# Up projection in fp32r: the input's two parts as one 512-column moving operand, with an earlier start of the down projection's loads

## The chip, the cores and the metric

One NeuronCore of one Trainium2 chip runs the whole block in one launch. The metric is the device time of the program in microseconds (us), as the median of several runs.

## The reference, cut to what matters

```
h    = rms_norm(x, norm2) * (1 + sc2) + sh2          # 512 tokens, 2048 channels
gate, val = split(h @ w_up, 2)                       # 2048 -> 2 x 6144
gate = causal_dwconv(gate, ffn_conv_w, ffn_conv_b)   # 3 taps along the tokens
x    = x + g2 * ((gelu(gate) * val) @ w_down)        # 6144 -> 2048
return rms_norm(x, norm_final)
```

Ahead of it stands a mixer of about the same kind (an input projection of 4096 columns, a gated token mixer, a linear recurrence, an output projection). The six modulation vectors (sh1, sc1, g1, sh2, sc2, g2) are products of `silu(c)` with `w_ada`.

## The kernel before, in words

All products run on TensorE in float32r. Each float32 operand is cut in two parts, `hi` (the value rounded to float32r) and `lo` (what is left), and a product is the sum of three: hi weights by hi input, hi weights by lo input, lo weights by hi input. `round_up` (line 162, ScalarE) writes the hi part of 1024 weight columns into `wh`, `rest` (line 167, VectorE) the lo part into `wl`; each tag has three buffers.

The program is a list `steps`. A step takes one 512 KB block of weights. The loop at the end of the kernel works at step j: it issues the load for step j + 5, rounds the weights of step j + 2 on ScalarE, runs the small work that `put(j, fn, cost, half)` has hung on the step (half -1 first, 0 before VectorE's rest for step j + 2, 1 after it), and issues the step's matmuls. Every engine keeps this order, so an instruction that waits holds up all that stand behind it on its engine.

Steps up to 95 are the mixer. Steps 96 to 111 make the first four output columns of the up projection in the plain way (`mm_w`, lines 173 to 175). The other 44 columns f (128 gate and 128 value channels each) are made by a Strassen-like scheme: 2 x 2 blocks of the weights and of the input (low and high channels, first and second 256 tokens) give seven products P1 to P7 in place of eight. So there are 308 steps. In each, `go` runs over eight blocks of 128 input channels, and for each over the three part products (lines 875 to 877) of 256 columns, one token half. The moving operand `m` has hi and lo side by side: for P1, P2 and P4 a half of each of the two rows of an `h2` tile (tag `hp`), for P6, P5, P7 and P3 sums of the blocks that `combine` (lines 818 to 840) made in steps 104 to 111, in tiles `xs` and `sx`. The results go to banks x, z and y of PSUM, all of them to the first half of the bank.

In `column(f)`, t1 to t4 (VectorE, lines 910 to 922) form sums of weight blocks, and `after_p1` to `after_p3` take the products out of the banks, 256 columns at a time: ScalarE copies c1, u2, u3 and half of the gate, VectorE adds z + c1 (938), y + u3 (948), y + u2 (956). Then come the taps (806), gelu (969), the product with the value (959), and the store of the 256 KB result to `kept`.

The down projection follows from step J1, in two halves of four groups of twelve steps; a step is 24 matmuls of 512 columns (5.44 us). Its input is read back: `act_load` (256 KB into `yl`, three buffers) and `act_split` (lines 1051 and 1052: hi on ScalarE, lo on VectorE) into 16 `hp` tiles and 11 `dp` tiles. `g2_load` fetches one 1 MB block of `w_ada` into the only `araw` buffer in every second step, and `ada` (line 209, VectorE) reduces it to one column of the gate g2. At a group's end `settle` (line 979, VectorE) adds the four finished banks, times g2, to x2. There are six banks for these sums, so the next group can start on two and needs settle for the rest. From step J1 + 4 the tiles `araw`, `yl` and `dp` stand in a pool `back`, in the order in which they are first asked for.

## Time and profile before

| what | value |
|---|---|
| median of 3 runs | 2150.6 us (2147.19 to 2150.71) |
| the profiled execution's own time | 2149.32 us |
| its span, first to last instruction | 2147.6 us |
| TensorE busy | 2094.9 us (98%) |
| weight loads busy | 1861.4 us (87%) |
| VectorE busy | 1508.0 us (70%) |
| ScalarE busy | 875.0 us (41%) |
| mean granted TensorE clock | 0.989 |

The profiled execution takes 1.7 us more than its span, and lies 1.3 us below the median. Matmuls overlap in the records (a row's length is longer than the distance to the next start), so TensorE's pace is read from the starts. The same holds in a small way for VectorE and ScalarE.

### The profile page before, as it was taken

The page shows a single profiled execution, that of the slowest core. Times are in us where ns is not written, and L with a number is a line of the kernel's source. Part 1 is how long each engine was busy: PE and PEld are TensorE (multiplying, and loading weights), DVE is VectorE, ACT ScalarE, POOL GpSimd, SP SyncE. Part 2 cuts the span into 40 slices and gives each one's busy share as a digit, 9 for nine tenths or more (in the row PEclk, how much of TensorE's full clock was granted, in tenths as well). Part 3 has the DMA queues.
Part 4 walks back from the last instruction along what each step waited for, and adds up shares of the span by engine and source line. Part 5 has one row for each costly group of instructions (what it writes and reads, how often), then busy time and mean ns, then how long its engine had stood idle before and what let it go on. Part 6 is the DMA issues. An engine that isn't in the chain of part 4 may idle for free. (4 is left out here: it accounts for less than half of the span.)

```text
span 2147.6 us, 30757 instructions
## 1 busy us (share of the span) xinstructions
PE 2094.9 (98%) x12620; PEld 1861.4 (87%) x12620; DVE 1508.0 (70%) x1851; ACT 875.0 (41%) x1148; POOL 4.7 (0%) x12
## 2 busy tenths in 40 slices
PE   7999999999989999999999999999998999999996
PEld 4887778888768999999999999999997888888885
DVE  8999889787768777877877877877865444432333
ACT  5323775332234544544544444444452112222222
POOL 0000000000000000000000000000000000000000
PEclk8999999999999999999999999999999999999998
DMA  9876443679822333233233233233256555422222
GB/s 369 331 286 222 147 157 129 225 285 336 301 96 99 126 131 131 93 132 128 94 133 127 95 133 127 95 133 127 96 182 258 217 210 182 160 91 98 89 98 79
DMA packets 97069, 351.43 MB, mean 164 GB/s; under 512 B 12704, under 2 KB 12832, under 8 KB 84640
## 3 DMA queue, kind: packets, MB, share of 16 engines
q1 hardware_dynamic: 81520, 293.36, 38.3%
q10 hardware_dynamic: 15408, 56.11, 7.2%
q8 instruction: 99, 1.62, 0.3%
q14 instruction: 42, 0.34, 0.0%
HBM read 328.45 MB, written 20.97 MB: 163 GB/s over the span
## 5 line engine op out<-in xcount | busy, mean ns | idle before, releaser
L162 ACT CAST wh<-raw 128x1024 fp32r<-128x1024 f32 x340 | 356.9, 1050 | 694.4 <-PE mm L174 483.8
L167 DVE TENSOR_TENSOR wl<-raw,wh 128x1024 fp32r<-128x1024 f32 x340 | 416.0, 1224 | 238.4 <-ACT wh L162 235.8
L173 PE MATMUL mm<-hp,wh 128*128 128x512 f32 x1280 | 508.7, 397 | 15.2 <-DVE xs L979 5.8
L175 PE MATMUL mm<-hp,wl 128*128 128x512 f32 x1280 | 502.2, 392 | 3.1 <-DVE wl L167 3.1
L174 PE MATMUL mm<-hp,wh 128*128 128x512 f32 x1280 | 502.5, 393 | 0.8 <-DVE hp L234 0.8
L173 PEld LDWEIGHTS mm<-hp,wh 128*128 128x128 f32 x1280 | 242.7, 190 | 72.4 <-ACT hp L226 9.1
L877 PE MATMUL mm<-xs,wl 128*128 128x256 f32 x1056 | 299.1, 283 | 0.6 <-DVE wl L167 0.5
L875 PE MATMUL mm<-xs,wh 128*128 128x256 f32 x1056 | 298.9, 283 | 0.0
L876 PE MATMUL mm<-hp,wh 128*128 128x256 f32 x1056 | 298.9, 283 | 0.0
L877 PE MATMUL mm<-hp,wl 128*128 128x256 f32 x1056 | 298.8, 283 | 0.0
L875 PE MATMUL mm<-hp,wh 128*128 128x256 f32 x1056 | 298.8, 283 | 0.0
L876 PE MATMUL mm<-xs,wh 128*128 128x256 f32 x1056 | 298.8, 283 | 0.0
L175 PEld LDWEIGHTS mm<-hp,wl 128*128 128x128 f32 x1280 | 242.5, 189 | 55.1 <-DVE wl L167 4.4
L174 PEld LDWEIGHTS mm<-hp,wh 128*128 128x128 f32 x1280 | 242.5, 189 | 54.3 <-issue 2.4
L209 DVE SCALAR_TENSOR_TENSOR araw<-araw,crow 128x2050 f32<-128x2050 f32 (+1 forms) x96 | 219.8, 2291 | 44.0 <-DMA araw<-w_ada 44.0
L167 DVE TENSOR_TENSOR wl<-rawb,wh 128x1024 fp32r<-128x1024 f32 x132 | 161.7, 1225 | 76.7 <-ACT wh L162 76.7
L877 PEld LDWEIGHTS mm<-xs,wl 128*128 128x128 f32 x1056 | 202.7, 192 | 1.0 <-DVE wl L167 1.0
L875 PEld LDWEIGHTS mm<-hp,wh 128*128 128x128 f32 x1056 | 202.7, 192 | 0.0
L875 PEld LDWEIGHTS mm<-xs,wh 128*128 128x128 f32 x1056 | 202.7, 192 | 0.0
L876 PEld LDWEIGHTS mm<-hp,wh 128*128 128x128 f32 x1056 | 202.7, 192 | 0.0
L877 PEld LDWEIGHTS mm<-hp,wl 128*128 128x128 f32 x1056 | 202.7, 192 | 0.0
L876 PEld LDWEIGHTS mm<-xs,wh 128*128 128x128 f32 x1056 | 202.7, 192 | 0.0
(214 smaller groups left out, 2615.5 us busy)
## 6 DMA issues: line engine op xcount, KB each, us to landing
araw<-w_ada SPq DMA_DIRECT2D x64, 1024.5 KB, 5.9
raw<-w_dn SPq DMA_DIRECT2D x96, 512.0 KB, 3.4
raw<-w_us SPq DMA_DIRECT2D x88, 512.0 KB, 4.5
rawb<-w_us SPq DMA_DIRECT2D x88, 512.0 KB, 4.9
araw<-w_ada SPq DMA_DIRECT2D x32, 1025.0 KB, 7.2
raw<-w_in ACTq DMA_DIRECT2D x59, 512.0 KB, 4.0
raw<-w_out ACTq DMA_DIRECT2D x32, 512.0 KB, 6.1
act_kept<-fy SPq DMA_DIRECT2D x48, 256.0 KB, 2.2
```

What stands on the lines that cost most here:

```text
L162: A.copy(hi, raw)
L167: V.tensor_tensor(out=lo, in0=raw, in1=hi, op=SUB)
L173: PE.matmul(ps, w[0][:, cs], h[0], start=first, stop=False)
L174: PE.matmul(ps, w[0][:, cs], h[1], start=False, stop=False)
L175: return PE.matmul(ps, w[1][:, cs], h[0], start=False, stop=last)
L209: V.scalar_tensor_tensor(out=raw, in0=raw, scalar=1.0, in1=crow[:, :w], op0=MUL, op1=MUL, accum_out=mods[:, n:n + 1])
L875: PE.matmul(ps, hi[:, cs], m[:, 0, :], start=first, stop=False, skip_group_check=True)
L876: PE.matmul(ps, hi[:, cs], m[:, 1, :], start=False, stop=False, skip_group_check=True)
L877: PE.matmul(ps, lo[:, cs], m[:, 0, :], start=False, stop=last, skip_group_check=True)
```

## The change

In a product, the hi weights now multiply both parts of the input in one matmul of 512 columns: hi input into the lower half of the bank, lo input into the upper half. The lo weights still multiply the hi input, 256 columns into the lower half. So 24 matmuls of 256 columns become 8 of 512 and 8 of 256. The two halves of a bank have to be added in the end; since the scheme is linear, that is done once per column and output: all copies and adds out of the banks are twice as wide (c1, u2, u3, `gw`, `vw`), `gate` adds the halves of the gate, `value` those of the value.

Of the four sums of `combine`, the fourth goes into the upper half of an `h2` tile, which is free once the plain steps have read it; the `sx` tiles go. For that reason the combines move one step later, and the last two share step 111.

In the down projection the first four loaded results are split into `xs` tiles, `yl` has four buffers, nearly every load is issued two steps ahead of its split where it was one, and the blocks of `w_ada` are loaded at steps J1 + 5, 7, 9, 11, 13, 16, 19 and so on in place of J1 + 4, 6, 8 and so on. The buffer `araw` grows by 128 bytes. The core of the diff (the renamed helpers of `column` that only got wider are left out):

```diff
-            raw = sb("araw", 2 if pl is mid else 1, (P, D + (2 if pl is mid else 32)), pl=pl)
+            raw = sb("araw", 2 if pl is mid else 1, (P, D + (2 if pl is mid else 64)), pl=pl)
...
-            two = sb("sx", 8, (P, 2, HS), F32R, ffn) if k in (2, 3) else sb("xs", NXS, (P, 2, HS), F32R)
+            two = sb("xs", NXS, (P, 2, HS), F32R) if i < 3 else h2[k][2][:, :, upper]
...
-            put(UP0 + 8 + k, lambda k=k, rests=rests: rests.append(combine(k)))
-            put(UP0 + 8 + k, lambda rests=rests: rests[0](), 0.0, 1)
+            j = UP0 + 9 + min(k, 6)
+            put(j, lambda k=k, rests=rests: rests.append(combine(k)))
+            put(j, lambda rests=rests: rests[0](), 0.0, 1)
...
-            ps = of[f][b][:, lower]
+            ps = of[f][b]
+            both = ps.rearrange("p (a b) -> p a b", a=2)
...
-                PE.matmul(ps, hi[:, cs], m[:, 0, :], start=first, stop=False, skip_group_check=True)
-                PE.matmul(ps, hi[:, cs], m[:, 1, :], start=False, stop=False, skip_group_check=True)
-                PE.matmul(ps, lo[:, cs], m[:, 0, :], start=False, stop=last, skip_group_check=True)
+                PE.matmul(both, hi[:, cs], m, start=first, stop=False, skip_group_check=True)
+                PE.matmul(ps[:, lower], lo[:, cs], m[:, 0, :], start=False, stop=last, skip_group_check=True)
...
-            V.tensor_tensor(out=o["g"][:, lower], in0=o["z"][:, lower], in1=o["c1"], op=ADD)
+            V.tensor_tensor(out=o["gw"][:, :, lower], in0=two(o["z"]), in1=two(o["c1"]), op=ADD)
...
-            V.tensor_tensor(out=o["v"][:, upper], in0=o["y"][:, lower], in1=u3, op=ADD)
+            V.tensor_tensor(out=o["vw"][:, :, upper], in0=two(o["y"]), in1=two(u3), op=ADD)
...
+        def gate():
+            o["g"] = sb("fg", 1, pl=ffn)
+            V.tensor_tensor(out=o["g"], in0=o["gw"][:, 0, :], in1=o["gw"][:, 1, :], op=ADD)
...
-            V.tensor_tensor(out=o["v"][:, lower], in0=o["y"][:, lower], in1=o["u2"], op=ADD)
+        def value():
+            V.tensor_tensor(out=o["vw"][:, 0, :], in0=o["vw"][:, 0, :], in1=o["vw"][:, 1, :], op=ADD)
...
+        put(at_["P4"] + 2, gate)
+        put(at_["P3"] + 3, value, 0.0, 1)
...
-        yls[f] = sb("yl", 3, pl=room2[0] or ffn)
+        yls[f] = sb("yl", 4, pl=room2[0] or ffn)
...
-        two = pair() if f < 16 or 27 <= f < 43 else sb("dp", 11, (P, 2, S), F32R, room2[0])
+        if f < EARLY:
+            hi, lo = (sb("xs", NXS, dt=F32R) for _ in range(2))
+        else:
+            two = pair() if f < EARLY + 16 or EARLY + 26 <= f < EARLY + 42 else sb("dp", 10, (P, 2, S), F32R, room2[0])
...
-        if f < 27:
+        if f < EARLY + 26:
             j = J1 + f // 2
-            first, then = (j - 3, j - 2) if f > 5 else (J1 + (-6, -6, -6, -3, -2, -1)[f], J1 + (-4, -3, -2, -1, 0, 0)[f])
+            first, then = (j - 4, j - 2) if f >= 8 else (J1 - 6, J1 - 2 + f // 2) if f < 4 else (J1 - 4 + f // 2, J1 - 2 + f // 2)
...
-        put(J1 + 4 + 2 * k, lambda k=k: g2_load(k))
-        put(J1 + 5 + 2 * k, lambda: ada(*g2_loaded.pop()))
+        j = J1 + (5 + 2 * k if k < 4 else 1 + 3 * k)
+        put(j, lambda k=k: g2_load(k))
+        put(j + (0 if k == 3 else 1), lambda: ada(*g2_loaded.pop()), 0.0, 1)
```

VectorE's order in one column of the up projection, from the add that follows P3 to the rest of the weights of the next column's P4 (`wl` and `wh` are parts of weights, `mm` banks, `vt` constants). Before:

```order
L956 TENSOR_TENSOR fv_5397<-mm_5342,u_902_5336 128x256
L167 TENSOR_TENSOR wl_5500<-raw_5206,wh_5498 128x1024
L922 TENSOR_TENSOR rawb_5322<-rawb_5322,t_916_5447 128x1024
L938 TENSOR_TENSOR fg_5530<-mm_5502,c_913_5429 128x256
L806 SCALAR_TENSOR_TENSOR fy_5464<-fg_5304,vt,fy_5464 128x511
L167 TENSOR_TENSOR wl_5535<-raw_5256,wh_5532 128x1024
L806 SCALAR_TENSOR_TENSOR fy_5464<-fg_5304,vt,fy_5464 128x510
L167 TENSOR_TENSOR wl_5568<-raw_5449,wh_5565 128x1024
L959 TENSOR_TENSOR fy_5464<-fy_5464,fv_5397 128x512
L167 TENSOR_TENSOR wl_5599<-rawb_5322,wh_5596 128x1024
```

Now:

```order
L960 TENSOR_TENSOR vw_5349<-mm_5310,u_894_5304 128x2x256
L964 TENSOR_TENSOR fg_5426<-gw_5280 128x512
L167 TENSOR_TENSOR wl_5430<-raw_5194,wh_5424 128x1024
L923 TENSOR_TENSOR rawb_5294<-rawb_5294,t_908_5387 128x1024
L946 TENSOR_TENSOR gw_5452<-mm_5432,c_905_5373 128x2x256
L167 TENSOR_TENSOR wl_5456<-raw_5244,wh_5454 128x1024
L806 SCALAR_TENSOR_TENSOR fy_5428<-fg_5426,vt,fy_5428 128x511
L806 SCALAR_TENSOR_TENSOR fy_5428<-fg_5426,vt,fy_5428 128x510
L167 TENSOR_TENSOR wl_5482<-raw_5389,wh_5479 128x1024
L969 TENSOR_TENSOR vw_5349<-vw_5349 128x512
L972 TENSOR_TENSOR fy_5428<-fy_5428,vw_5349 128x512
L167 TENSOR_TENSOR wl_5506<-rawb_5294,wh_5503 128x1024
```

The three bank adds are two times 256 wide where they were 256, and the adds of lines 964 and 969 are new, so the same stretch has twelve instructions in place of ten.

VectorE's order where the plain steps end and the columns begin, from the rest of P2's weights in step 111 (`rawb` holds sums, line 838 makes their lo parts, `t` is a sum of weight blocks, and line 806 is a tap of the last two plain columns). Before:

```order
L167 TENSOR_TENSOR wl_5190<-rawb_5111,wh_5175 128x1024
L915 TENSOR_TENSOR t_885_5204<-rawb_5064,raw_4970 128x1024
L838 TENSOR_TENSOR xs_5182<-rawb_5177,xs_5182 128x256
L838 TENSOR_TENSOR xs_5184<-rawb_5177,xs_5184 128x256
L838 TENSOR_TENSOR xs_5186<-rawb_5177,xs_5186 128x256
L838 TENSOR_TENSOR xs_5188<-rawb_5177,xs_5188 128x256
L806 SCALAR_TENSOR_TENSOR fy_5224<-mm_4860,vt,fy_5224 128x511
L806 SCALAR_TENSOR_TENSOR fy_5224<-mm_4860,vt,fy_5224 128x510
```

Now:

```order
L167 TENSOR_TENSOR wl_5178<-rawb_5089,wh_5152 128x1024
L916 TENSOR_TENSOR t_877_5192<-rawb_5043,raw_4951 128x1024
L838 TENSOR_TENSOR xs_5159<-rawb_5154,xs_5159 128x256
L838 TENSOR_TENSOR xs_5161<-rawb_5154,xs_5161 128x256
L838 TENSOR_TENSOR xs_5163<-rawb_5154,xs_5163 128x256
L838 TENSOR_TENSOR hp_4611<-rawb_5154,hp_4611 128x256
L838 TENSOR_TENSOR xs_5171<-rawb_5166,xs_5171 128x256
L838 TENSOR_TENSOR xs_5173<-rawb_5166,xs_5173 128x256
L838 TENSOR_TENSOR xs_5175<-rawb_5166,xs_5175 128x256
L838 TENSOR_TENSOR hp_4614<-rawb_5166,hp_4614 128x256
L806 SCALAR_TENSOR_TENSOR fy_5216<-mm_4847,vt,fy_5216 128x511
L806 SCALAR_TENSOR_TENSOR fy_5216<-mm_4847,vt,fy_5216 128x510
```

Eight lo parts stand ahead of the taps in place of four, and four more instructions of a combine stand ahead of the first row.

VectorE's order at the end of the first group of the down projection (`dp` are split results, `araw` a block of `w_ada`, and the `xs` rows are settle). Before:

```order
L1052 TENSOR_TENSOR dp_15852<-yl_15832,dp_15852 128x512
L1052 TENSOR_TENSOR dp_15855<-yl_15834,dp_15855 128x512
L167 TENSOR_TENSOR wl_15860<-raw_15722,wh_15848 128x1024
L1052 TENSOR_TENSOR dp_15892<-yl_15874,dp_15892 128x512
L209 SCALAR_TENSOR_TENSOR araw_15858,mods<-araw_15858,crow 128x2049
L167 TENSOR_TENSOR wl_15896<-raw_15765,wh_15888 128x1024
L979 SCALAR_TENSOR_TENSOR xs_15662<-mm_15430,mods,xs_15662 128x512
L979 SCALAR_TENSOR_TENSOR xs_15706<-mm_15431,mods,xs_15706 128x512
```

Now:

```order
L209 SCALAR_TENSOR_TENSOR araw_13483,mods<-araw_13483,crow 128x2049
L1072 TENSOR_TENSOR dp_13560<-yl_13499,dp_13560 128x512
L1072 TENSOR_TENSOR dp_13563<-yl_13501,dp_13563 128x512
L167 TENSOR_TENSOR wl_13568<-raw_13432,wh_13556 128x1024
L209 SCALAR_TENSOR_TENSOR araw_13566,mods<-araw_13566,crow 128x2049
L994 SCALAR_TENSOR_TENSOR xs_13329<-mm_13097,mods,xs_13329 128x512
L994 SCALAR_TENSOR_TENSOR xs_13372<-mm_13098,mods,xs_13372 128x512
L994 SCALAR_TENSOR_TENSOR xs_13416<-mm_13099,mods,xs_13416 128x512
L994 SCALAR_TENSOR_TENSOR xs_13459<-mm_13100,mods,xs_13459 128x512
L1072 TENSOR_TENSOR dp_13603<-yl_13539,dp_13603 128x512
L1072 TENSOR_TENSOR dp_13606<-yl_13541,dp_13606 128x512
```

The splits of the group's end now stand behind settle, and the fourth block of `w_ada` is reduced right ahead of it, in the step of its load.

## Rows read from the trace of the kernel before

**Rows 1.** The page: busy us, share of the span, instructions.

```profile
PE 2094.9 (98%) x12620; PEld 1861.4 (87%) x12620; DVE 1508.0 (70%) x1851; ACT 875.0 (41%) x1148; POOL 4.7 (0%) x12
```

**Rows 2.** Busy time by stretch, up projection: stretch, length, engines, granted clock, DMA.

```profile
900.00:1100.00 200.00, 200.00 (x1669) 200.00 (x1668) 157.93 (x169) 98.64 (x130) 0.00 (x0) 1.00 0.34 117
```

**Rows 3.** Order of time, TensorE, up projection (101 matmuls): start, length, line, tiles.

```profile
1000.06 0.28 PE L877 MATMUL mm<-hp,wl 128*128 128x256 f32 x1
...
1012.06 0.28 PE L875 MATMUL mm<-xs,wh 128*128 128x256 f32 x1
```

**Rows 4.** The same, down projection: 25 matmuls on dp, then 16 on hp.

```profile
1640.25 0.40 PE L173 MATMUL mm<-dp,wh 128*128 128x512 f32 x1
...
1645.85 0.40 PE L173 MATMUL mm<-dp,wh 128*128 128x512 f32 x1
...
1799.89 0.39 PE L175 MATMUL mm<-hp,wl 128*128 128x512 f32 x1
...
1803.29 0.39 PE L175 MATMUL mm<-hp,wl 128*128 128x512 f32 x1
```

**Rows 5.** Groups by line, 650:1650 (last: 40:560): count, busy us, mean ns, idle before.

```profile
L162 ACT CAST wh<-raw 128x1024 fp32r<-128x1024 f32 x152 | 159.6, 1050 | 130.0 <-PE mm L876 103.0 <-issue 13.1 <-PE mm L174 12.7
L167 DVE TENSOR_TENSOR wl<-raw,wh 128x1024 fp32r<-128x1024 f32 x151 | 184.2, 1221 | 5.4 <-ACT wh L162 3.2
L814 DVE TENSOR_TENSOR fy<-mm,fy 128x512 f32<-128x512 f32 x4 | 2.8, 692 | 4.3 <-ACT fy L813 4.3
L332 ACT COPY xs<-mm 128x512 f32<-128x512 f32 x16 | 8.9, 588 | 1.6 <-PE mm L182 0.5 <-PE mm L175 0.4
```

**Rows 6.** Order of time, VectorE, within one column.

```profile
1007.81 0.42 DVE L938 TENSOR_TENSOR fg<-mm,c 128x256 f32<-128x256 f32 x1
```

**Rows 7.** Order of time where the columns begin: VectorE, last row TensorE.

```profile
691.26 0.48 DVE L825 SCALAR_TENSOR_TENSOR rawb<-xs,shsum,xs 128x256 f32<-128x256 f32 x1
...
695.24 1.42 DVE L838 TENSOR_TENSOR xs<-rawb,xs 128x256 fp32r<-128x256 f32 x4
696.58 1.53 DVE L806 SCALAR_TENSOR_TENSOR fy<-mm,vt,fy 128x511 f32<-128x511 f32 x2
...
702.76 1.23 DVE L167 TENSOR_TENSOR wl<-t,wh 128x1024 fp32r<-128x1024 f32 x1 [0.25 <-ACT wh L162]
...
704.04 0.39 PE L877 MATMUL mm<-xs,wl 128*128 128x256 f32 x1 [0.49 <-DVE wl L167]
```

**Rows 8.** Order of time, TensorE after two earlier waits (rows 549.28 to 553.28: 12 matmuls).

```profile
549.28 0.50 PE L173 MATMUL mm<-hp,wh 128*128 128x512 f32 x1 [2.70 <-DVE xs L382]
...
553.28 0.62 PE L175 MATMUL mm<-hp,wl 128*128 128x512 f32 x1
...
587.15 0.50 PE L175 MATMUL mm<-hp,wl 128*128 128x512 f32 x1 [1.69 <-DVE wl L167]
```

**Rows 9.** Busy time by stretch, right after the second of these waits.

```profile
587.00:589.00 2.00, 1.85 (x8) 1.54 (x9) 1.84 (x3) 0.00 (x0) 0.00 (x0) 1.00 0.38 115
```

**Rows 10.** Order of time, first group of the down projection: TensorE, ScalarE, VectorE.

```profile
1647.23 0.50 PE L175 MATMUL mm<-dp,wl 128*128 128x512 f32 x1 [0.74 <-DVE wl L167]
...
1653.61 0.39 PE L175 MATMUL mm<-hp,wl 128*128 128x512 f32 x1
1659.84 0.79 PE L173 MATMUL mm<-hp,wh 128*128 128x512 f32 x1 [5.85 <-DVE xs L979]
...
1663.28 0.39 PE L175 MATMUL mm<-hp,wl 128*128 128x512 f32 x1
...
1654.43 0.62 ACT L1051 CAST dp<-yl 128x512 fp32r<-128x512 f32 x1 [7.12 <-DMA yl<-act_kept]
...
1655.69 2.29 DVE L209 SCALAR_TENSOR_TENSOR araw<-araw,crow 128x2049 f32<-128x2049 f32 x1
...
1659.04 2.72 DVE L979 SCALAR_TENSOR_TENSOR xs<-mm,mods,xs 128x512 f32<-128x512 f32 x4
```

**Rows 11.** DMA issues, 1600 to 1900 us: queue, count, KB each, median us to landing.

```profile
araw<-w_ada SPq DMA_DIRECT2D x16, 1024.5 KB, 5.9
```

More of the change, by code (lines that the diff above doesn't have):

```diff
@@ L927, in column, with copied, two, wide @@
         put(max(at_["P6"] - 1, at_["P2"] - 2), t4, 0.0, 1)
-        def half(tag):
-            return sb(tag, 1, (P, HS), pl=ffn)
+        def copied(tag):
+            t = sb(tag, 1, pl=ffn)
+            A.copy(t, o["x"])
+            return t
+        def two(t):
+            return t.rearrange("p (a b) -> p a b", a=2)
+        def wide(tag):
+            return sb(tag, 1 + (tag == "vw"), (P, 2, S), pl=ffn)
         def after_p1():
-            o["c1"] = half("c1")
-            A.copy(o["c1"], o["x"][:, lower])
+            o["c1"] = copied("c1")
@@ L936, in after_p2 @@
         def after_p2():
-            o["g"] = sb("fg", 2, pl=ffn)
-            V.tensor_tensor(out=o["g"][:, lower], in0=o["z"][:, lower], in1=o["c1"], op=ADD)
+            o["gw"] = wide("gw")
+            V.tensor_tensor(out=o["gw"][:, :, lower], in0=two(o["z"]), in1=two(o["c1"]), op=ADD)
         def after_p6():
-            o["u2"] = half("u2")
-            A.copy(o["u2"], o["x"][:, lower])
+            o["u2"] = copied("u2")
         def after_p7():
-            u3 = half("u3")
-            A.copy(u3, o["x"][:, lower])
@@ L947, in after_p7, with after_p3 @@
-            o["v"] = sb("fv", 2, pl=ffn)
-            V.tensor_tensor(out=o["v"][:, upper], in0=o["y"][:, lower], in1=u3, op=ADD)
+            u3 = copied("u3")
+            o["vw"] = wide("vw")
+            V.tensor_tensor(out=o["vw"][:, :, upper], in0=two(o["y"]), in1=two(u3), op=ADD)
         def after_p4():
-            A.copy(o["g"][:, upper], o["x"][:, lower])
+            A.copy(o["gw"][:, :, upper], two(o["x"]))
+        def after_p3():
+            V.tensor_tensor(out=o["vw"][:, :, lower], in0=two(o["y"]), in1=two(o["u2"]), op=ADD)
@@ L1049, in act_split @@
         y = yls.pop(f)
-        two = pair() if f < 16 or 27 <= f < 43 else sb("dp", 11, (P, 2, S), F32R, room2[0])
-        A.copy(two[:, 0, :], y)
-        V.tensor_tensor(out=two[:, 1, :], in0=y, in1=two[:, 0, :], op=SUB)
-        act[f] = (two[:, 0, :], two[:, 1, :], two)
+        if f < EARLY:
+            hi, lo = (sb("xs", NXS, dt=F32R) for _ in range(2))
+        else:
+            two = pair() if f < EARLY + 16 or EARLY + 26 <= f < EARLY + 42 else sb("dp", 10, (P, 2, S), F32R, room2[0])
+            hi, lo = two[:, 0, :], two[:, 1, :]
+        A.copy(hi, y)
+        V.tensor_tensor(out=lo, in0=y, in1=hi, op=SUB)
+        act[f] = (hi, lo)
     def second_room():
```

14 lines of the change are left out of this document (7 added, 7 removed).

## The prediction

> **What bounds the kernel now.** I began with the page: TensorE is busy for 98% of the span [rows 1], so time comes or goes only where TensorE's pace or its few waits change. The stretches show where the other engines stand during the up projection [rows 2]: TensorE never idles, at the full granted clock, VectorE is busy for 157.93 of 200 us, ScalarE for 98.64. Then the order of time on TensorE, for its pace. In the up projection 101 matmuls of 256 columns start in 12.00 us [rows 3]: 0.1200 us each. In the down projection 16 matmuls of 512 columns on `hp` start in 3.40 us, 0.2267 us each, and 25 on `dp` in 5.60 us, 0.2333 us each [rows 4]. The reader is to see that 256 columns more cost 0.1067 us, which is 256 cycles at the level of 2.4 GHz, and that both widths carry the same 13.3 ns on top. The kernel pays this 24 times per product. The other views are of the two places where TensorE waits: the beginning of the columns [rows 7] and the end of the first group of the down projection [rows 10].
>
> **The change, part by part. The products.** A product was 24 matmuls of 0.1200 = 2.880 us. It becomes 8 of 0.2267 and 8 of 0.1200 = 2.774 us; the columns streamed are the same, and eight times 13.3 ns go. For 44 columns of 7 products, 308 x 0.1064 = **32.8 us less**. No row shows wide and narrow matmuls in turns. The bounds: nothing gained, if a narrow one behind a wide one takes 0.133 us, and 32.8. I take 32.8, since both rows fit one fixed amount per matmul. A smaller doubt: for P1, P2, P4 and P3 the wide operand is two separate runs of 256. If that cost what `dp` costs over `hp` [rows 4], 4 x 8 x 44 = 1408 matmuls would lose 6.6 ns each, 9.3 us. I take nothing, as the hi and the lo run are each read at full pace today.
>
> The Trainium skill (TensorE: Matmul & The Clock Gate, "Wait — 56ns, not 53.3ns?") gives a back-to-back matmul a fixed cost of about 2.5 ns. By that figure the 2464 matmuls saved would be worth 6.2 us, not 32.8; this case's rows show 13.3 ns at both widths, so the sum goes by the rows.
>
> **What the wider outputs cost.** A VectorE row overlaps the next by 0.08 us (four adds of 1.42 us are followed after 1.34 [rows 7]). A bank add of 512 takes 0.69 us [rows 5] in place of 0.42 [rows 6]: three times 0.27 = 0.8 us. The adds in `gate` and `value` cost 0.61 each. VectorE thus goes from 157.93/200 x 20.16 = 15.9 us per column to 17.9, and a column from 7 x 2.880 = 20.16 us to 19.42: 92% busy. ScalarE's four copies go from about 0.4 us each to 0.59 [rows 5], from 9.9 us per column to about 11. What hides this is that weights are prepared two steps ahead (5.55 us). I followed one column from the start of its P1, with 1.05 for a rounding, 1.14 for a rest or a weight sum [rows 5] and 0.6 for a copy or an add. In the first step (copy, rounding, rest, t1) VectorE is done at 4.0. In the second, from 2.8, copy and rounding end at 4.4, rest and t2 at 6.8. ScalarE's rounding of t2 lets VectorE begin the rest of P6's weights at 7.9, and from there VectorE runs through: rest 1.14, t3 1.14, bank add 0.6, gate 0.6, rest for P5 1.14 (done at 12.5, due at 13.9), t4 1.14, bank add 0.6, rest for P7 1.14. That one ends at 15.4 and is due at 16.6. This margin of 1.2 us is the smallest, and the column ends with 1.5 us to spare, so nothing piles up. I cost the wider work at **nothing**; with the margin gone, each us of lateness would cost 44 us.
>
> **Where the columns begin.** The last two combines now share step 111. VectorE gets four more instructions of about 0.48 us, 1.7 us in all, and four more lo parts, 695.24 to 696.58 = 1.3 us, ahead of the taps that start at 696.58 [rows 7]. Behind these wait two taps, a gelu, a product, the same once more, ScalarE's rounding of t2, and at 702.76 the rest of P6's weights, for which TensorE waits already (0.49 us). So all 3.0 us come on the path. TensorE would stand still for some 2.9 us. After an idle of 2.70 us the chip granted half the clock (1.2 GHz): the 12 matmuls from 549.28 to 553.28 took 4.00 us for 11 distances, in place of 2.49 [rows 8]. After 1.69 us [rows 8] it stayed at 1.00 [rows 9]. I add 1.5 us: **4.5 us more**, between 0 (VectorE caught up earlier) and 6.
>
> **The down projection's first group.** At 1653.61 TensorE has used its two free banks and waits until settle [rows 10]. VectorE reaches settle at 1659.04, because it stood behind a split whose load landed late (ScalarE waited 7.12 us for `yl`) and a reduction of 2.29 us. The loss: 0.74 us of an earlier wait, 6.23 less one distance = 6.0, and at half clock 10 distances in 3.44 us in place of 2.27 = 1.2. That is 7.9 us. Now the loads have two steps and four buffers, so no split should wait. What is late next is the fourth block of `w_ada`: the third is reduced in step 10, after the rounding (1.05) and the rest (1.22) [rows 5], until 4.5 us from that step's start. Then its buffer is free, the fourth block lands 5.9 us later [rows 11], at 10.4, is reduced until 12.7, and the first settle (2.72/4 = 0.7) ends at 13.4. The group ends at 10.9, and TensorE's two free banks last 6 matmuls, to 12.2. A wait of about 1.1 us is left, too short for the clock. **6.8 us less**, between 0 (the loads get in each other's way) and 7.9.
>
> **The place of dp.** 16 results pass through `dp`, each used by 48 matmuls: 768 times 6.6 ns = 5.0 us. In the pool the old order is 8320 bytes of `araw`, three `yl` of 2048, then `dp`, 128 bytes past a multiple of 256 from the pool's start; now it is four `yl` and 8448 bytes, a multiple of 256, as `sx` had from the same start, and `sx` was read at the pace of `xs`. No row proves that the place is what makes `dp` slow, so the bounds are 0 and 5.0. I take **5.0 us less**, for no other difference between `dp` and `hp` is seen.
>
> **The sum**, against the profiled execution's own 2149.3 us: - 32.8 + 4.5 - 6.8 - 5.0 = - 40.1, so **2109 us**. The median lies 1.3 us above that execution, which is within the spread of the runs. 0.2% of it, 4.3 us, is about what a measurement can tell from no change.
>
> **The rivals.** (1) The pace of TensorE hardly changes: the 13.3 ns belong to the change of weights in a stream of equal widths, and a narrow matmul behind a wide one takes up to 0.133 us. Weight loads are busy without a gap [rows 2], which speaks for it; that wide matmuls, with far more time per load, carry the same 13.3 ns [rows 4] speaks against it. Without the 32.8 us the sum is 2142; with a tenth to a fifth of it, 2135 to 2139. The Trainium skill's figure (TensorE: Matmul & The Clock Gate) would make it this case.
>
> (2) VectorE becomes the bound, and the kernel slower. Before, VectorE idled 42.07 of 200 us [rows 2], 4.2 us per column, in waits for ScalarE's rounding, which waits for TensorE to free a weight buffer. If these waits stay while the work grows to 17.9 us, a column takes 22.1 us in place of 20.16, and 44 columns 85 us more: 2149 + 85 - 7 = about 2227. It decides from 2.3 us of such waits per column on. Against it: they are waits of an engine that runs ahead, and my column keeps 1.2 us. For half of it (VectorE binds, but by less), the time lies between 2127 and 2146.
>
> (3) The earlier loads don't do what they are for: the wait at the first group's end stays, 2116.
>
> **How the numbers follow.** The forecast with its smaller terms either way, rival (3) in it, has 0.80. Low end: no loss where the columns begin and all of 7.9 us, 2149.3 - 32.8 - 7.9 - 5.0 = 2103.6, and 2.6 for the spread of the runs: 2101. High end: 32.8 us gained, but 6 lost and neither of the two smaller gains, 2122.5, and half of the 9.3 us for the split operand: 2127. Rival (1) has 0.07, the half form of (2) 0.08, both faster but for 0.01; rival (2) in full 0.05. So faster 0.94, no change 0.01, slower 0.05.
>
> **What would show it.** In the profile after: starts 0.227 and 0.120 us in turns, a product every 2.774 us, and VectorE near 92% in a stretch of the columns; a wait of 3 to 4 us on TensorE before P6 of the first column, with a granted clock below 1.00 behind it; one short wait, or none, at the first group's end; `dp` at 0.227. I am wrong if TensorE's waits for `wl` recur in every column, if the narrow starts are further apart than 0.125, or if 9 us are missing in the products on `hp`.

## The result, and the profile after

The changed kernel takes 2128.7 us in the median of 4 runs (2116.2 to 2133.1), the kernel before 2150.5 beside it (2147.2 to 2150.7): a ratio of 0.9893, 95% interval 0.9849 to 0.9936. It is faster, by about half of what was forecast, and lies above the range of 2101 to 2127. The four runs are 17 us apart, those of the kernel before 3.5; this turned out to be the clue.

The profiled execution takes 2133.12 us, 16.2 less than the one before; its span, 2131.2 us, is 16.4 shorter. By stretches of the span: up to the first column 697.3 before, 700.8 now (+3.5; this stretch differs from run to run, 692.7 to 700.8 in the 17 profiles of the changed kernel and its variants); the columns 888.2 and 875.9 (-12.3); the down projection to the end 562.1 and 554.5 (-7.6). The forecast had -28.3 for the columns and -11.8 for the down projection.

The columns first. The page's busy line and the stretch that answers to [rows 2] (stretch, length, PE, PEld, DVE, ACT, POOL, granted clock, DMA share, GB/s):

```profile
PE 2074.0 (97%) x10156; PEld 1729.5 (81%) x10156; DVE 1590.0 (75%) x1939; ACT 907.9 (43%) x1148; POOL 4.6 (0%) x12
```

```profile
900.00:1100.00 200.00, 200.00 (x1134) 173.54 (x1133) 180.65 (x192) 107.14 (x133) 0.00 (x0) 1.00 0.34 122
```

TensorE doesn't idle, at the full clock; VectorE is busy for 180.65 of 200 us and no row of TensorE waits for it. So the pace itself is short of the forecast. The order of time on TensorE, where [rows 3] stood before:

```profile
999.72 0.40 PE L877 MATMUL mm<-hp,wh 128*128 128x512 f32 x1
999.96 0.28 PE L878 MATMUL mm<-hp,wl 128*128 128x256 f32 x1
1000.08 0.40 PE L877 MATMUL mm<-hp,wh 128*128 128x512 f32 x1
...
1002.20 0.40 PE L877 MATMUL mm<-hp,wh 128*128 128x512 f32 x1
1002.44 0.28 PE L878 MATMUL mm<-hp,wl 128*128 128x256 f32 x1
1002.55 0.40 PE L877 MATMUL mm<-hp,wh 128*128 128x512 f32 x1
```

Seven pairs of a wide and a narrow matmul from 999.72 to 1002.20 give 0.354, and over the 2441 pairs behind the wait at the beginning of the columns it is 0.3533 us a pair, the same for products on `hp` and on `xs`; the forecast had 0.2267 + 0.1200 = 0.3467. The 6.7 ns between them (16 cycles at the level of 2.4 GHz) make 308 x 8 x 6.67 ns = 16.4 us. Half of the expected gain is not there. Read to the nanosecond, the trace shows a pattern: from a wide start to the narrow one behind it, 236, 233 and 241 ns, over and over to the end of the columns, so three pairs (1.060 us) make one round.

At the beginning of the columns VectorE's order and TensorE's wait are as forecast (compare [rows 7]; TensorE's first wait ends with ScalarE's copy `c`, which stands behind the gelu and the rounding of t2). The stretch behind it shows the clock:

```profile
703.06 1.53 DVE L806 SCALAR_TENSOR_TENSOR fy<-mm,vt,fy 128x511 f32<-128x511 f32 x2
...
709.24 1.23 DVE L167 TENSOR_TENSOR wl<-t,wh 128x1024 fp32r<-128x1024 f32 x1 [0.25 <-ACT wh L162]
```

```profile
709.74 0.50 PE L877 MATMUL mm<-xs,wh 128*128 128x512 f32 x1 [3.10 <-ACT c L932]
710.51 0.58 PE L878 MATMUL mm<-xs,wl 128*128 128x256 f32 x1 [0.27 <-DVE wl L167]
```

```profile
710.00:713.00 3.00, 2.73 (x9) 2.20 (x9) 3.00 (x4) 1.68 (x2) 0.00 (x0) 0.53 1.00 329
```

TensorE stands for 3.4 us and then runs at half clock (1.2 GHz; 0.53 granted from 710 to 713 us). That is 4.1 us more than the kernel before lost here: the columns are 12.3 us shorter where their pairs alone would make them 16.4 shorter. At the end of the first down group, where [rows 10] stood, a wait of 4.16 us is left, and on VectorE its cause:

```profile
1642.92 0.39 PE L174 MATMUL mm<-xs,wh 128*128 128x512 f32 x1
1643.14 0.39 PE L175 MATMUL mm<-xs,wl 128*128 128x512 f32 x1
1647.69 0.50 PE L173 MATMUL mm<-xs,wh 128*128 128x512 f32 x1 [4.16 <-DVE xs L994]
```

```profile
1635.10 2.29 DVE L209 SCALAR_TENSOR_TENSOR araw<-araw,crow 128x2049 f32<-128x2049 f32 x1
...
1644.67 2.30 DVE L209 SCALAR_TENSOR_TENSOR araw<-araw,crow 128x2049 f32<-128x2049 f32 x1 [4.04 <-DMA araw<-w_ada]
...
1646.88 2.72 DVE L994 SCALAR_TENSOR_TENSOR xs<-mm,mods,xs 128x512 f32<-128x512 f32 x4
```

The third block was reduced until 1637.4; the fourth was asked for right then, at 1637.42, and its reduction began at 1644.67, 7.25 us later (a load took 5.9 before, [rows 11]). Settle waits for it.

`dp` is now read at the pace that `hp` had, as forecast: ten matmuls start in 2.27 us, 0.227 each, where [rows 4] had 0.2333.

```profile
1639.74 0.39 PE L175 MATMUL mm<-dp,wl 128*128 128x512 f32 x1
...
1642.01 0.39 PE L173 MATMUL mm<-xs,wh 128*128 128x512 f32 x1
```

### The profile page after: what moved, and what is told of

The parts are those of the page before. It is cut to its first block, busy times and chain, and to the rows that moved or that the text cites. A ratio compares the mean times of both kernels' runs of the same rounds, so it can differ in the third digit from the quotient of the medians.

```text
span 2131.2 us, 26094 instructions
## 1 busy us (share of the span) xinstructions
PE 2074.0 (97%) x10156; PEld 1729.5 (81%) x10156; DVE 1590.0 (75%) x1939; ACT 907.9 (43%) x1148; POOL 4.6 (0%) x12
## 5 line engine op out<-in xcount | busy, mean ns | idle before, releaser
L173 PE MATMUL mm<-hp,wh 128*128 128x512 f32 x1280 | 507.1, 396 | 10.4 <-ACT hp L226 5.5
L174 PE MATMUL mm<-hp,wh 128*128 128x512 f32 x1280 | 501.0, 391 | 0.8 <-DVE hp L234 0.8
L877 PE MATMUL mm<-hp,wh 128*128 128x512 f32 x1408 | 499.5, 399 | 0.0
L878 PE MATMUL mm<-hp,wl 128*128 128x256 f32 x1408 | 395.5, 281 | 0.0
L877 PE MATMUL mm<-xs,wh 128*128 128x512 f32 x1056 | 376.4, 400 | 3.1 <-ACT c L932 3.1
L877 PEld LDWEIGHTS mm<-hp,wh 128*128 128x128 f32 x1408 | 264.6, 188 | 66.0
L173 PEld LDWEIGHTS mm<-hp,wh 128*128 128x128 f32 x1280 | 241.8, 189 | 67.5 <-ACT hp L226 9.1
L175 PEld LDWEIGHTS mm<-hp,wl 128*128 128x128 f32 x1280 | 241.6, 189 | 59.6 <-DVE wl L167 9.3
L174 PEld LDWEIGHTS mm<-hp,wh 128*128 128x128 f32 x1280 | 241.7, 189 | 53.8 <-issue 2.4
L878 PEld LDWEIGHTS mm<-hp,wl 128*128 128x128 f32 x1408 | 266.1, 189 | 0.0
L877 PEld LDWEIGHTS mm<-xs,wh 128*128 128x128 f32 x1056 | 199.2, 189 | 53.1 <-ACT c L932 3.4
L162 ACT CAST wh<-rawb 128x1024 fp32r<-128x1024 f32 x132 | 138.3, 1047 | 7.6 <-issue 4.4
L167 DVE TENSOR_TENSOR wl<-t,wh 128x1024 fp32r<-128x1024 f32 x44 | 53.9, 1225 | 50.6 <-ACT wh L162 50.6
L932 ACT COPY u<-mm 128x512 f32<-128x512 f32 x88 | 51.7, 587 | 89.2 <-PE mm L878 89.2
L173 PE MATMUL mm<-dp,wh 128*128 128x512 f32 x192 | 75.2, 392 | 0.0
```

What stands on the lines that cost most here:

```text
L162: A.copy(hi, raw)
L167: V.tensor_tensor(out=lo, in0=raw, in1=hi, op=SUB)
L173: PE.matmul(ps, w[0][:, cs], h[0], start=first, stop=False)
L174: PE.matmul(ps, w[0][:, cs], h[1], start=False, stop=False)
L175: return PE.matmul(ps, w[1][:, cs], h[0], start=False, stop=last)
L877: PE.matmul(both, hi[:, cs], m, start=first, stop=False, skip_group_check=True)
```

## The experiments

The question was the pair: 0.3533 or 0.3467 us, and why. The first theory: the change of width is not free, and what it costs differs between executions. Its rivals: the wide operand of the columns is slow in itself, or other parts of the change cost the time. Below, "pair" means the distance between two starts of wide matmuls, square brackets hold the 95% interval, and ratios are to runs of the kernel before on the same chip. Only the profiled execution of each kernel shows its pace; of the others there is the time alone.

**1. The changed kernel again (again).** No edit.

> The changed kernel once more, unaltered. Its four times lay from 2116.15 to 2133.12 us, while those of the kernel before lay within 3.5 us. Theory A (the pace differs between executions): a wide and a narrow matmul together start every 0.3533 us in slow executions (as in the trace at hand) and every 0.3467 us in the fast ones, worth 2464 x 6.7 ns = 16.4 us, so the times fall into two heaps some 16 us apart. Theory B (the pair always takes 0.3533): the products give only 16.4 us, and the spread comes from the stage before the columns; then all times lie within about 10 us, and the low one is an exception of the mixer's waits.

2131.0 us in the median of 6 runs (2113.7 to 2133.0), ratio 0.9901 [0.9876, 0.9925]. The profiled execution, at 2113.7, shows the forecast's pace:

```profile
900.00:1100.00 200.00, 200.00 (x1156) 174.92 (x1155) 183.60 (x198) 109.55 (x134) 0.00 (x0) 1.00 0.33 119
```

1156 matmuls in place of 1134. It waits at the same two places, 3.10 us at the beginning of the columns and 6.07 at the first group's end (3.10 and 4.16 in the first profile), so it isn't faster by shorter waits. The order of time, ahead of the wait at the beginning of the columns and later:

```profile
698.46 0.40 PE L877 MATMUL mm<-hp,wh 128*128 128x512 f32 x1
...
699.88 0.40 PE L877 MATMUL mm<-hp,wh 128*128 128x512 f32 x1
...
1000.37 0.39 PE L877 MATMUL mm<-xs,wh 128*128 128x512 f32 x1
...
1001.76 0.39 PE L877 MATMUL mm<-xs,wh 128*128 128x512 f32 x1
```

Four pairs take 1.42 us ahead of the wait, 1.39 behind it (0.3527 over the 15 pairs ahead, 0.3467 over the 2437 behind). So both paces exist, in one kernel and nearly so in one execution. At 0.3467 the round of three pairs is gone: 230 to 233 ns from every wide start to the narrow one. Of ten timed executions of the changed kernel two were at 2114 to 2116 us, eight at 2127 to 2133: theory A's two heaps, though only one execution of each was profiled.

**2. Four wide, then four narrow (grouped).**

```diff
-                m = MOVING[p](k)
...
+                PE.matmul(both, hi[:, cs], MOVING[p](k), ...)
+            for k in range(4 * kk, 4 * kk + 4):
+                cs = slice(k % 4 * P, k % 4 * P + P)
...
-                PE.matmul(both, hi[:, cs], m, ...)
-                PE.matmul(ps[:, lower], lo[:, cs], m[:, 0, :], ...)
+                PE.matmul(ps[:, lower], lo[:, cs], MOVING[p](k)[:, 0, :], ...)
```

> In each half product the four wide matmuls first, then the four narrow ones. If the extra 6.7 ns belong to a change of width (theory C), a product pays it two times in place of eight: 2.774 + 0.013 to 0.027 us, 12 to 15 us less than the changed kernel in the same state. If each wide matmul of the columns costs it by itself, as its operand has two parts (theory D), a product stays at 2.827 us and the time too.

2125.3 us (2119.0 to 2132.5, 5 runs), ratio 0.9887 [0.9869, 0.9905]. Eight changes of width become two per half product, and the half product takes 1.40 us (1002.91 to 1004.31), a product 2.807: between the two paces in turns (2.774, 2.827), and above what theory C had (2.787 to 2.801).

```profile
1002.91 1.09 PE L875 MATMUL mm<-xs,wh 128*128 128x512 f32 x4
1003.83 0.64 PE L879 MATMUL mm<-xs,wl 128*128 128x256 f32 x4
1004.31 1.09 PE L875 MATMUL mm<-xs,wh 128*128 128x512 f32 x4
```

**3. All but the wide matmul (narrow).** Three matmuls of 256 columns as before, everything else as changed.

```diff
-                PE.matmul(both, hi[:, cs], m, ...)
+                PE.matmul(ps[:, lower], hi[:, cs], m[:, 0, :], ...)
+                PE.matmul(ps[:, upper], hi[:, cs], m[:, 1, :], ...)
```

> All of the change but the wide matmul: hi input into the lower half and lo input into the upper half of the bank by two matmuls of 256 columns, 24 per product. All theories: starts 0.1200 us apart, 2.880 us per product, so 308 x (2.880 - 2.827) = 16 us more than the changed kernel's trace, some 2149 us; if 2.774 is what a fast execution has, 33 us more than that. A time of 2128 would say that the pace of TensorE is not what the columns' time hangs on.

2147.7 us (2143.7 to 2151.2, 10 runs), ratio 0.9987 [0.9977, 0.9997]. The rest of the change together is worth 2.6 us; the columns' gain is the wide matmul's alone (without it they take 892.1 us, 3.9 more than before, by the wait at their beginning). Behind that wait the twice as wide copies and adds make TensorE wait nowhere. The runs are 7.5 us apart, not 19, and the profile has one pace, 0.1200 a matmul.

**4. The combines sooner (early).** The first two combines share a step instead of the last two.

```diff
-            j = UP0 + 9 + min(k, 6)
+            j = UP0 + 8 + max(k, 1)
```

> Combines 0 and 1 share a step (105) in place of 6 and 7 (111), so VectorE has the instructions of one combine less ahead of the last plain taps. My account of the beginning of the columns (3.0 us of work on the path and 1.5 us at half clock) says about 4 us less than the changed kernel, the wait of 3.10 us before P6 of the first column gone, and the granted clock 1.00 there. If VectorE loses as much at step 105, nothing changes.

2128.6 us (2126.6 to 2130.9, 4 runs), ratio 0.9898 [0.9884, 0.9913]. Of the 3.4 us at the beginning of the columns 0.45 are left, about what the kernel before had there (0.49):

```profile
703.60 0.28 PE L878 MATMUL mm<-hp,wl 128*128 128x256 f32 x1
704.04 0.50 PE L877 MATMUL mm<-xs,wh 128*128 128x512 f32 x1 [0.17 <-ACT c L932]
```

But the pair was 0.3533 in the profile, the wait at the first group's end 7.13 us, and no run was below 2126. So that term was rightly named, but it is a small one beside the pace.

**5. Eight wide, then eight narrow (parts).** A product's wide matmuls go to its first half, the narrow ones to its second.

```diff
-            for k in range(4 * kk, 4 * kk + 4):
+            for k in range(KT // 2):
+                hi, lo = ws[j][k // 4]
...
-                PE.matmul(both, hi[:, cs], m, ...)
-                PE.matmul(ps[:, lower], lo[:, cs], m[:, 0, :], ...)
+                if kk == 0:
+                    PE.matmul(both, hi[:, cs], m, ...)
+                else:
+                    PE.matmul(ps[:, lower], lo[:, cs], m[:, 0, :], ...)
```

> The changed kernel with the order of the 16 matmuls of a product changed: its eight wide ones in the first half, its eight narrow ones in the second. In the changed kernel a pair of a wide and a narrow matmul took 0.3533 us in most executions and 0.3467 in one; grouped by four and four, a product took about 2.807 us. Theory A (the extra time belongs to the change of width, and whether it is paid differs from one execution to the next): two changes of width per product are left of sixteen, so a product takes 2.774 to 2.79 us in every execution, the time is 2112 to 2119 us, and the runs lie closer together than the 19 us of the changed kernel. Theory B (the wide matmul on the columns' operand, two runs of 256 numbers, takes 0.2333 to 0.2367 whatever stands beside it): a product stays at 2.827 us or above it, and the time at 2127 to 2133.

2120.9 us (2115.4 to 2121.7, 4 runs), ratio 0.9857 [0.9842, 0.9872]. A product takes 2.793 us:

```profile
1002.67 2.00 PE L879 MATMUL mm<-xs,wh 128*128 128x512 f32 x8
1004.51 1.11 PE L881 MATMUL mm<-xs,wl 128*128 128x256 f32 x8
1005.46 1.78 PE L879 MATMUL mm<-xs,wh 128*128 128x512 f32 x7
```

The runs are 6 us apart. The product stands just above theory A's 2.774 to 2.79, the time above its 2112 to 2119; the profile had a wait of 5.3 us at the first group's end. Against the slower pace in turns (53 ns above 2.774 a product), grouped pays 33 ns and parts 20, so there fewer changes of width cost less. But at the faster pace sixteen changes cost nothing, so the number of changes alone does not set the price. In parts the 20 ns stand behind the narrow matmuls: the next wide ones start 233, 236, 228, 232 and 231 ns apart before 226.7 is reached.

**6. All matmuls wide (wide16).** The lo weights multiply both parts too, one part product more.

```diff
-                PE.matmul(ps[:, lower], lo[:, cs], m[:, 0, :], ...)
+                PE.matmul(both, lo[:, cs], m, ...)
```

> The changed kernel with the rest of the weights multiplying both parts too (16 matmuls of 512 columns per product, one product more in the sum than the reference needs), so that no width changes within a product. Theory A (the change of width costs): each matmul takes 0.2267 us as on hp in the down projection, a product 3.627 us, the time about 2129 + 308 x 0.80 = 2375 us. Theory B (the columns' wide operand costs): 0.2333 to 0.2367 each, a product 3.73 to 3.79, the time 2408 to 2425 us.

2375.2 us (2373.9 to 2377.0, 3 runs), as forecast by theory A. On `xs` the operand is one run of 512, on `hp` it is two runs of 256. Three distances on `xs` from 999.84 to 1000.52 and fifteen on `hp` from 1001.88 to 1005.28 give 0.227 each: the operand in two runs is read at full pace. The rival falls.

```profile
999.84 0.39 PE L878 MATMUL mm<-xs,wl 128*128 128x512 f32 x1
1000.06 0.39 PE L877 MATMUL mm<-xs,wh 128*128 128x512 f32 x1
...
1000.52 0.39 PE L877 MATMUL mm<-xs,wh 128*128 128x512 f32 x1
...
1001.88 0.39 PE L877 MATMUL mm<-hp,wh 128*128 128x512 f32 x1
...
1005.28 0.39 PE L878 MATMUL mm<-hp,wl 128*128 128x512 f32 x1
```

**7. The w_ada blocks sooner (sooner).**

```diff
-        j = J1 + (5 + 2 * k if k < 4 else 1 + 3 * k)
+        j = J1 + (4 + 2 * k if k < 4 else 1 + 3 * k)
         put(j, lambda k=k: g2_load(k))
-        put(j + (0 if k == 3 else 1), lambda: ada(*g2_loaded.pop()), 0.0, 1)
+        put(j + 1, lambda: ada(*g2_loaded.pop()), 0.0, 0 if k in (2, 3) else 1)
```

> The changed kernel with the first four w_ada blocks of the down projection loaded a step sooner, and the third and the fourth reduced ahead of the rest of the weights. Theory A (the wait of 4.5 to 6.5 us at the end of the first group is the chain of four loads and reductions through one buffer, which begins too late): the fourth reduction ends before the group does, the wait there is under 1 us, the clock stays at 1.00, and 5 to 7 us of the changed kernel's time go: 2122 to 2125 us. Theory B (the loads are late because the DMA engines are shared with the other loads of that stretch, and each sooner load only lands later): the fourth block still lands more than 6.5 us after it is asked for, a wait of 2 us or more stays, and the time is within 2 us of 2129.

2118.9 us (2110.4 to 2128.3, 6 runs), ratio 0.9853 [0.9827, 0.988]. The fourth block lands 5.8 us after it is asked for (1617.65), is reduced before the group ends, and TensorE waits 1.24 us in place of 4.16:

```profile
1623.48 2.30 DVE L209 SCALAR_TENSOR_TENSOR araw<-araw,crow 128x2049 f32<-128x2049 f32 x1 [1.14 <-DMA araw<-w_ada]
...
1626.84 2.72 DVE L994 SCALAR_TENSOR_TENSOR xs<-mm,mods,xs 128x512 f32<-128x512 f32 x4
```

```profile
1627.64 0.50 PE L173 MATMUL mm<-xs,wh 128*128 128x512 f32 x1 [1.24 <-DVE xs L994]
```

The wait is a little longer than theory A had, but theory B falls: the sooner load landed faster, not later. The chain through one buffer was the cause; the edit moves its loads and two of its reductions at once, so it doesn't say how much each is worth. The six times fall into two clumps, 2110 to 2114 and 2123 to 2128, each some 4 us below the changed kernel's; the profile, at 2111.6, has 0.3467, and that the upper clump is the other pace is read from the times.

**8. parts, early and sooner together (joined).**

> Three edits of the changed kernel together: wide matmuls first and narrow ones second in a product, the first two combines in one step instead of the last two, and the w_ada blocks of the first down group a step sooner. If theory A holds for the pace and for the loads, no wait over 1 us is left at the beginning of the columns and at the end of the first group, a product takes 2.774 to 2.79 us, and the time is 2103 to 2110 us, some 20 us below the changed kernel. If neither holds: 2125 to 2130, as the kernel with the combines alone.

2112.6 us (2112.1 to 2115.4, 5 runs), ratio 0.9828 [0.9815, 0.9841]: some 2.5 us above what was expected, with a wait of 1.1 us left at the first group's end. A product takes 2.793 us. The runs are 3.3 us apart, the least of all the faster versions.

**9. Waits on purpose (jolts).** early and sooner together, and work of no use on VectorE that makes TensorE wait in fourteen columns.

```diff
+        for _ in range(JOLT.get(f, 0)):
+            put(place["P6", f], lambda: V.tensor_tensor(out=crow, in0=crow, in1=crow, op=mybir.AluOpType.max))
```

> The changed kernel with the first two combines in one step and the w_ada blocks a step sooner, so that TensorE comes into the columns without a long wait, and with work of no use on VectorE (a maximum of a tile with itself, some 2.2 us each) in fourteen columns, one such instruction in the columns 7 to 25, every third, and two in the columns 28 to 46; each makes TensorE wait, the two for longer. In the profiles so far the 15 pairs ahead of the wait at the beginning of the columns took 0.3527 us in every execution, and behind that wait 0.3467 in some and 0.3533 in others, until the columns end. Theory R (TensorE's pace in alternating widths is drawn anew when it starts again after a wait, and then stays): the pace between two waits is 0.3533 behind some of the fourteen and 0.3467 behind others. Theory C (only a start at half clock draws anew): the pace stays at 0.3533 through the first seven, and changes behind some of the last seven, if the granted clock falls there. Theory E (something of the whole execution sets it): one pace throughout.

One execution (2150.1 us, the waits included). Of the stretches between two waits, the last two of the short ones and the first three of the long ones (matmuls started in 50 us: 290 is a pair of 0.3467, 285 of 0.3533; at a short wait two wide matmuls start 1.5 us apart, at a long one 3.5 to 4.0):

```profile
1070.00:1120.00 50.00, 50.00 (x290) 44.08 (x289) 45.97 (x50) 27.82 (x35) 0.00 (x0) 1.00 0.40 143
1130.00:1180.00 50.00, 50.00 (x285) 43.40 (x284) 45.34 (x49) 27.24 (x34) 0.00 (x0) 1.00 0.39 143
1196.00:1246.00 50.00, 50.00 (x285) 43.41 (x284) 44.52 (x47) 26.27 (x33) 0.00 (x0) 1.00 0.38 135
1260.00:1310.00 50.00, 50.00 (x285) 43.39 (x284) 44.52 (x47) 26.19 (x32) 0.00 (x0) 1.00 0.36 134
1325.00:1375.00 50.00, 50.00 (x290) 44.08 (x289) 44.69 (x48) 27.27 (x34) 0.00 (x0) 1.00 0.37 132
```

The pace changes at waits and only there (the shortest, near the end of the columns, held TensorE up by 0.1 us); between two of them, three columns apart, it is constant. It changed behind the last of the seven short waits, through which the clock stayed at 1.00, so a start at half clock is not needed (theory C falls); behind six short waits it did not change. Theory E falls too. Ahead of the short wait at the beginning of the columns (0.17 and 0.29 us) it was 0.3527, behind it 0.3467.

**10. Cuts (kicks).** early and sooner together; one narrow matmul in fourteen columns is cut in two.

```diff
+    KICK = dict(zip(range(7, 47, 3), (8, 16, 24, 32, 40, 48, 64, 80, 96, 128, 8, 16, 32, 64)))
...
+                c = KICK.get(f, 0) if p == "P1" and k == 1 else 0
+                if c:
+                    PE.matmul(ps[:, :c], lo[:, cs], m[:, 0, :c], ...)
-                PE.matmul(ps[:, lower], lo[:, cs], m[:, 0, :], ...)
+                PE.matmul(ps[:, c:HS], lo[:, cs], m[:, 0, c:], ...)
```

> The same kernel without the work of no use, and with one narrow matmul of the first product in fourteen columns (7 to 46, every third) cut in two, of 8, 16, 24, 32, 40, 48, 64, 80, 96, 128, 8, 16, 32, 64 columns and the rest, so that the alternation is broken without a wait. Theory R in its narrower form (any break in the alternation draws the pace anew): the pace behind the cuts is 0.3467 in some columns and 0.3533 in others, and the same size of cut gives the same pace in its second place if the place of the start within a fixed beat decides. Rival (only standing still does): 0.3533 throughout, as ahead of the first cut.

One execution (2114.0 us). The pace changes at cuts too, without any wait. Cuts of 16, 24, 32 and 40 columns, and the stretches of 50 us behind them:

```profile
814.00:864.00 50.00, 50.00 (x290) 44.10 (x289) 45.09 (x48) 27.32 (x34) 0.00 (x0) 1.00 0.36 131
872.00:922.00 50.00, 50.00 (x284) 43.37 (x284) 44.51 (x48) 27.05 (x33) 0.00 (x0) 1.00 0.35 132
932.00:982.00 50.00, 50.00 (x291) 43.73 (x290) 45.01 (x49) 27.35 (x35) 0.00 (x0) 1.00 0.35 127
990.00:1040.00 50.00, 50.00 (x285) 43.35 (x284) 44.50 (x47) 27.21 (x33) 0.00 (x0) 1.00 0.36 131
```

Nine of the fourteen stretches ran at 0.3467. Equal cuts gave equal paces for 8, 16 and 64, not for 32.

**11. early and sooner, without cuts (both).**

> The changed kernel with the first two combines in one step and the w_ada blocks a step sooner, the pairs left in turns. Without a long wait ahead of the columns, theories R and C leave TensorE at the pace with which it begins, 0.3533 us a pair, in every execution: 2121 to 2126 us (2128.6, as with the combines alone, less 4 to 6 for the first group), with runs as close together as those of the kernel with the combines alone (4.3 us). Theory E: one execution in three or four at 0.3467, 2105 to 2110, and a spread of some 18 us.

2117.4 us (2103.4 to 2127.2, 6 runs), ratio 0.9834 [0.9797, 0.9871]. The spread of 24 us is a miss for what I wrote under theories R and C: two runs at 2103 to 2104, two at 2126 to 2127, two at 2117. The short wait at the beginning of the columns was enough to change the pace in jolts. In experiment 4, with the same short wait, all four times lay at 2127 to 2131; that this was chance is likely, but not shown. The two runs at 2117 were only timed, and what they did isn't known.

**12 to 14. One cut in every column (cut8, cut16, cut64).** The edit of 10 with the same size in all 44 columns.

> The kernel with the combines and the w_ada blocks sooner, and in each of the 44 columns one narrow matmul of the first product cut into 8 and 248 columns. Theory S (the size of the cut sets the pace behind it, and 8 sets 0.3467): every column runs at 0.3467 us a pair, the time is 2103 to 2108 us (the two fastest runs of the kernel without cuts, 2103.4 and 2104.2, and 44 more matmuls at 0.03 to 0.06 us), and the runs lie within 6 us of one another. Theory D (each cut is a draw by chance, nine of fourteen were 0.3467): the columns mix, the mean pair is about 0.349, the time 2108 to 2113 with runs closer together than the 24 us without cuts. Rival N (nothing new: one pace per execution): 2104 or 2125.

> As before, with cuts of 16 and 240 columns. Theory S: every column at 0.3467, 2103 to 2108 us. Theory D: mixed columns, 2108 to 2113 us.

> As before, with cuts of 64 and 192 columns. Theory S: every column at 0.3467, 2103 to 2108 us, or, as two of two by chance are no rare thing, another fixed pace than for 8. Theory D: mixed columns, 2108 to 2113 us.

cut8: 2116.3 us (2110.7 to 2118.8, 4 runs), ratio 0.9845 [0.9827, 0.9863]; cut16: 2110.1 (2107.1 to 2114.2, 5 runs), 0.9824 [0.9808, 0.984]; cut64: 2125.6 (2120.3 to 2128.8, 5 runs), 0.9889 [0.9873, 0.9904]. In cut8 the columns go fast, fast, slow, over and over to the end (30 fast, 15 slow stretches); stretches of 18 us in five columns in a row:

```profile
709.00:727.00 18.00, 18.00 (x106) 15.87 (x105) 15.72 (x17) 9.66 (x12) 0.00 (x0) 1.00 0.15 55
729.00:747.00 18.00, 18.00 (x104) 15.62 (x103) 16.48 (x18) 9.20 (x12) 0.00 (x0) 1.00 0.34 126
748.50:766.50 18.00, 18.00 (x106) 15.73 (x105) 16.02 (x18) 9.59 (x12) 0.00 (x0) 1.00 0.34 122
768.00:786.00 18.00, 18.00 (x106) 15.86 (x106) 16.24 (x19) 9.61 (x12) 0.00 (x0) 1.00 0.37 128
787.50:805.50 18.00, 18.00 (x105) 15.62 (x104) 16.21 (x19) 9.62 (x12) 0.00 (x0) 1.00 0.36 129
```

In cut16 all of them are at 0.3467 from the second cut on; in cut64 all are at 0.3535 but one. That is no chance from cut to cut (theory D falls). Nor does the size alone set the pace (theory S): 8 leads to both. It reads as if a cut moved the alternation by a fixed amount within some beat, and the pace followed from where it then stands; this is not shown. A beat is there to be read, though: in the twelve profiles with wide and narrow in turns, every one of the 76 stretches of 20 pairs or more at the slower pace repeats after three pairs, as in the changed kernel (233, 241 and 236 ns from wide to narrow, within 2), and none of the 99 at the faster pace does (230 to 232 in the mean). A cut costs about 0.1 us (0.449 from wide to wide across it in cut16, in place of 0.347), 4 to 5 us in all.

**15, 16. Three cuts at the beginning (after16, few16).** Cuts of 16 in columns 5, 6 and 7 alone, in the changed kernel and in that of 11.

> The changed kernel with one narrow matmul of the first product cut into 16 and 240 columns in the sixth, seventh and eighth column of the feed-forward part (5, 6, 7) and nowhere else. If the cut of 16 sets the pace and it lasts: 0.3467 us a pair from there to the end of the columns in the profile and in every execution, 2111 to 2117 us (the two fastest runs of the changed kernel were 2113.7 and 2116.2), with the runs some 6 us apart instead of 19. If the cut is a draw by chance, or the pace falls back by itself: as the changed kernel, most runs at 2127 to 2133.

> The same three cuts in the kernel with the first two combines in one step and the w_ada blocks a step sooner. If the cut sets the pace and it lasts: 0.3467 us a pair behind the third cut, 2102 to 2107 us (cut16, 2110.1, less 41 cuts at 0.12 us), within 8 us of one another. If not: 2103 to 2127 from run to run, as without the cuts.

after16: 2114.6 us (2111.7 to 2127.3, 5 runs), ratio 0.9835 [0.981, 0.9861]. Four of five runs were at 2112 to 2118; the profiled one, at 2127.3, kept 0.3533 through all three cuts. few16: 2106.3 us (2104.0 to 2110.4, 5 runs), ratio 0.9789 [0.9775, 0.9803], the fastest version; its profile shows 0.3467 already ahead of the first cut, and to the end of the columns. So a cut of 16 keeps the faster pace wherever it was seen (47 times), and of four that met the slower one a single one led out of it (the second of cut16). That all five times of few16 lie near 2106 is likely owed to the cuts, but this is not shown.

## Why the prediction was wrong

**The products (the step that failed).** The prediction took "32.8, since both rows fit one fixed amount per matmul". The direction is right: fewer matmuls, fewer fixed amounts, and no other engine in the way (experiment 3: without the wide matmul nothing of the columns' gain is there). The term was mis-sized, since the fixed amount of a stream of one width was carried over to widths in turns: 13.3 ns per matmul hold in a stream of one width (0.1200 in narrow, 0.2267 in wide16), while widths in turns settle at 0.3467 or at 0.3533 a pair. At the first the term is 32.8, at the second 16.4, and by their times eight of ten executions of the changed kernel were at the second. Which one an execution gets was not forecast and is not explained. Rival (1) put the loss on a narrow matmul behind a wide one and was given 0.07; by the rows it stands ahead of the narrow start (0.2364 us from wide to narrow in the mean at the slower pace, 0.2317 at the faster), while a wide one follows a narrow one after 0.117 and 0.115. So the sign of narrow starts over 0.125 apart did not come, though half of the gain was missing; that of 9 us missing on `hp` did (1408 x 6.7 ns), but `xs` lost as much in each pair. A half gain had no chance of its own, though the prediction itself said that no row shows wide and narrow in turns. So its smaller doubt, the operand in two runs, was not it; wide16 reads both in 0.227.

The rows speak against the figure of the Trainium skill (TensorE: Matmul & The Clock Gate, "Wait — 56ns, not 53.3ns?"), about 2.5 ns per back-to-back matmul: wide16 starts 512 columns every 0.2267 us, 13.3 ns above 512 cycles at the level of 2.4 GHz. By that figure the term would, as an estimate, have been 6.2 us; it was 16.4 in the profiled execution and 32.8 in that of experiment 1.

**What the wider outputs cost: right.** VectorE was busy for 180.65 of 200 us, 17.9 us per column of 19.79, as worked out (17.8 of 19.41 at the faster pace, experiment 1), and TensorE waited for it nowhere behind the beginning of the columns. Rival (2) did not come about.

**Where the columns begin: right.** 4.1 us more lost, 4.5 forecast; with the combines sooner the wait is gone (experiment 4).

**The first group: wrong by more than half.** 2.6 us gained in place of 6.8 (what is left of the down projection's 7.6 behind the 5.0 of `dp`). The prediction had the third block reduced 4.5 us into its step; it took 6.2, since the sum left out the two splits that stand ahead on VectorE and wait 2.4 us for ScalarE's halves, and the load of the fourth took 7.25 us in place of 5.9. Together that is 3.0 us, the difference between the 1.1 forecast and the 4.16 that TensorE waited. Experiment 7 confirms the chain. Rival (3), that the wait stays, is more than half true.

**The place of dp: right in size.** 0.227 where it was 0.2333: 5.0 us. That the place is the reason is not shown: no run moves `dp` alone.

The sum as measured, - 16.4 + 4.1 - 2.6 - 5.0 = - 19.9, and + 3.5 from the stretch ahead of the columns, is the - 16.4 of the span. With 32.8 in place of 16.4 and without the 3.5 the execution of 2133.1 would have taken 2113 us; the one that is known to have had that pace took 2113.7.

## What to carry to other kernels

Where instructions of two lengths will stand in turns for the first time, rows of each length alone gave only the best case here: give the mixture its own case with a chance, or put equal lengths together, which here (eight and eight) cost 6 us against the best pace and gave times 3 to 6 us apart. Where a kernel's runs lie much further apart than those of its neighbour, look for something that differs between executions; here two profiles, one from each end of the times, named it. And a chain of loads through one buffer carries the delay of every link to its end: write down all that stands ahead of each link on its engine, and begin the chain sooner than the sum says.
